# A small projection done in fp32 during the choice of experts, with another place for the seeds of the sums and another order of the weight ring

## The chip, the cores and the metric

The kernel runs on one core of a Trainium2 chip. The metric is the time of one execution on the device in microseconds (us); lower is better. The engines are TensorE (PE; its weight loads are PEld), VectorE (DVE), ScalarE (ACT), GpSimd (POOL) and SyncE (SP), which issues most of the weight transfers.

## What is computed

Two blocks act one after the other on 256 tokens of width 1024, all in fp32: a hybrid block (state-space mixer and block attention, then a mixture of experts, then a gate by a per-layer embedding), and a block of RWKV and convolution with a feed-forward layer. The part that the change touches:

```python
# x: after the mixer.  32 experts in 4 groups of 8, two chosen in a token's group
h = rms_norm(x, moe_norm_w)
x = x + hier_moe(h, w_router_group, b_router_group, w_router_expert,
                 b_router_expert, w_exp_gate, w_exp_up, w_exp_down)
gate = sigmoid(rms_norm(x, ple_norm_w) @ w_ple_gate)     # 1024 -> 1024
x = x + gate * (p @ w_ple)                               # p: 256 x 256, w_ple: 256 x 1024
return rms_norm(x, final_norm_w)
```

`p @ w_ple` depends on inputs alone.

## The kernel before

Most dense products are made in three passes. A weight piece of 512 KB (128 partitions x 1024 fp32) is loaded by `fetch` through SP's queue into a buffer `raw`; `split` makes a high half `whi` on ScalarE (L238) and the rest `wlo` on VectorE (L239); PE multiplies hi by hi, lo by hi and hi by lo in the faster fp32r form (L266, L284). Only products of plain fp32 tiles, such as transposes, gathers, the router and the experts, go to PE unsplit.

The program is written stage by stage, and a tile scheduler sets each engine's queue from that order, the buffers and the dependences. Each engine then runs its queue in order.

`mix1` is the first mixer. Its last product writes X1, the residual (256 tokens in two halves of 128); `hT_chunk` transposes it into two tiles `hT`. `route` multiplies hT by the router's weights `wr` (L794), chooses group and experts on VectorE (ending in `sel`, L819), and counts the tokens per expert with small matmuls on PE (the rank matmuls, L847). `moe` goes over 8 groups of 4 experts: `gather` makes a selection matrix `Pm` (L946) and collects 32 tokens for each expert with 32 matmuls (L955) into `xg`; 64 matmuls (L986) make gate and up; silu and product; 32 matmuls (L1007) make the down product; `slots` (L965) makes the weights `PT`, by which L1015 adds the results to four PSUM sums `acc`. These sums begin with X1 itself: four fp32 matmuls of X1 with the identity, the seeds (L938). After the gate and up products of the first group, all engines branch around `overflow` (L861), which is for an expert with more than 32 tokens; it isn't taken here.

The experts' weights are 192 pieces of 512 KB, 16 of gate and up and 8 of down for each group, taken from HBM in the order of use. `expert_fetch` (L911) puts piece n into buffer n modulo 40 of a ring, `self.ring`. The first 38 pieces (`NFIRST`) are issued ahead of the router, each when the buffer's earlier user is done: the `mw` buffers at P12 and P6 of the mixer's order `PROG1`, the rest of 38 at the start of `moe`. From piece 38 on a piece is issued where its user stands in the program, and waits for its buffer:

```python
n.ring = [(mw, "mw")] * NEARLY + [(None, "a8")] * 16 + [(raw, "raw")] * 4
n.ring += [(wsp, "whi"), (wsp, "wlo")] * 3 + [(mw, "mw")] * 2
```

After the experts, X1 is taken from the sums (L1023) and squared (L304). `ple` transposes it into `xh` and `xl` (L377, L378), calls `ple_proj`, which splits p and w_ple and makes U = p @ w_ple with 24 fp32r matmuls (L1045), and multiplies by `w_pg` (`toks`, 8 pieces of 12 matmuls, L284); sigmoid, product with U and sum follow (L1069 to L1071), then the norm into the second block.

Of the kernel before, what the change touches and what calls it, by code (L numbers as in the profile page):

```python
# [9 lines left out]
F32 = mybir.dt.float32  # L10
# [157 lines left out]
class Net:  # L168
# [524 lines left out]
    def mix1(self):  # L693
# [41 lines left out]
        for c in range(2):  # L735
# [9 lines left out]
            self.hT_chunk(X1, c)  # L745
        self.X1 = X1
# [40 lines left out]
    def route(self, hT, r):  # L787
# [4 lines left out]
        for tt in range(2):  # L792
            for kt in range(8):
                PE.matmul(ps[:, tt, :], hT[kt // 4][:, kt % 4, tt * 128:tt * 128 + 128], wr[:, kt, :], start=(kt == 0),  # L794
                          stop=(kt == 7))
        L = self.c1.tile([128, 2, 36], F32, name="L")
# [59 lines left out]
    def overflow(self, acc, comb, rank, cnti):  # L856
# [4 lines left out]
        with tc.If(cv > 32):  # L861
# [6 lines left out]
            hT = self.hT  # L868
            gu, pt = [self.bank(tag="B") for _ in range(2)], self.bank((128, 256), "B")
            with tc.For_i(0, 8) as q:  # L870
                for e in range(4):
                    for kt in range(8):
                        w = self.t2(s="wf")
                        nc.gpsimd.dma_start(w, a["w_gu"][bass.ds(q, 1), kt, e // 2, :, e % 2, :].rearrange("o p n -> (o p) n"))
                        for tt in range(2):
                            PE.matmul(gu[tt], hT[kt // 4][:, kt % 4, tt * 128:tt * 128 + 128], w, start=(kt == 0), stop=(kt == 7))
# [47 lines left out]
    def moe(self):  # L924
# [3 lines left out]
        self.expert_early(NFIRST - self.wi)  # L928
# [5 lines left out]

        acc = [[self.bank(tag="A", s="acc") for _ in range(2)] for _ in range(2)]
        for h in range(2):
            for tt in range(2):
                PE.matmul(acc[tt][h], self.ident, X1[:, tt, 512 * h:512 * h + 512], start=True, stop=False,  # L938
                          skip_group_check=True)
# [37 lines left out]
        nxt = gather(0)  # L977
        for q in range(8):
# [9 lines left out]
            if q == 0:  # L988
                self.overflow(acc, comb, rank, cnti)
                PT = slots(q, Pm)  # L990
# [27 lines left out]
        self.p = self.t2((128, 2, 256), s="p")  # L1018
        nc.sync.dma_start(self.p, a["pT"])
# [9 lines left out]
    def ple_proj(self):  # L1029
# [3 lines left out]
        self.U = U = self.a8(shape=(128, 2, 1024), s="U")  # L1033
        ph, pl = (self.t2((128, 2, 256), F32R, s="ps") for _ in range(2))
        S.activation(ph, self.p, AF.Copy)
        V.tensor_sub(pl, self.p, ph.bitcast(F32))
        for c in range(2):
            hi, lo = self.split(self.fetch(a["w_ple"][c]))
            for tt in range(2):
                ts = slice(128 * tt, 128 * tt + 128)  # L1040
                ps = self.bank(tag="B")
                n = 0
                for kt in range(2):
# [676 lines left out]
```

## Time and profile before

| | us |
|---|---|
| median of 3 runs | 1257.74 (1257.6 to 1259.7) |
| the profiled execution | 1260.09 |
| its span, first to last instruction | 1258.4 |
| PE busy | 1131.2 |
| VectorE busy | 745.1 |
| ScalarE busy | 511.5 |

The rows further down are from the profiled execution; its times count from the first instruction. Its mean granted TensorE clock is 0.955 of full speed. Matmuls overlap in PE, so a row's duration is longer than the distance to the next one, and an fp32 matmul can stand as two records.

### The profile page before, as it was taken

To read this page: it belongs to the slowest core of one execution; us is meant where nothing else is said; L and a number is where in the kernel's file an instruction comes from. 1 tells how busy PE (TensorE), PEld (TensorE's weight loads), DVE (VectorE), ACT (ScalarE), POOL (GpSimd) and SP (SyncE) were. 2 spreads that over 40 slices of the span, in tenths; PEclk is the share of its full clock that TensorE was granted. 3 is DMA by queue.
4 is the path that set the end of the run, shared out by engine and by line. 5 is a ranking of instruction groups with operands and counts; after the bars stand their busy time and mean duration, and the time that the engine had idled before them with its cause. 6 is when DMAs were issued, how large, how long until landed. Compare 5 with 4: busy or idle time off the path is not lost.

```text
span 1258.4 us, 20687 instructions
## 1 busy us (share of the span) xinstructions
PE 1131.2 (90%) x8211; PEld 887.1 (70%) x8211; DVE 745.1 (59%) x1513; ACT 511.5 (41%) x881; POOL 119.7 (10%) x126
## 2 busy tenths in 40 slices
PE   5999999999979988878789899998749999999996
PEld 5988976667754433216687798887736797999995
DVE  4777677656532111106846799889884366656555
ACT  4643644544411000006536535556215335545453
POOL 0002330001000000000200501014200000000000
PEclk9999999999979999998889899998857999999998
DMA  8743555327769999994353365122420136555552
GB/s 300 277 162 104 155 179 167 120 98 288 272 258 409 409 409 409 409 408 146 116 184 132 98 183 157 52 93 84 150 60 2 35 108 233 179 189 191 189 187 99
DMA packets 82981, 242.26 MB, mean 193 GB/s; under 512 B 24160, under 2 KB 24416, under 8 KB 82496
## 3 DMA queue, kind: packets, MB, share of 16 engines
q1 hardware_dynamic: 80224, 231.11, 51.3%
q0 software_dynamic: 2224, 8.90, 2.6%
q8 instruction: 66, 1.08, 0.4%
q10 hardware_dynamic: 432, 0.89, 0.2%
q14 instruction: 35, 0.29, 0.1%
HBM read 234.31 MB, written 4.46 MB: 190 GB/s over the span
## 4 chain that ended last, share of the span: by engine, by line
PE 47%; DVE 11%; DMA 5%; ACT 3%; issue 2%; POOL 1%; DVEq 0%; ACTq 0%; POOLq 0%; SPq 0%
PE ps L266 17%; PE acc L284 7%; DVE cv L1454 4%; PE ps L986 3%; PE ps L1007 3%; DMA we<-in_w_gu 3%; PE ps L284 2%; DVE wlo L239 2%; PE ps L1586 2%; PE ps L955 2%; DMA we<-in_w_dn 2%; PE acc L1015 2%; PE ps L1304 1%; ACT whi L238 1%; PE ps L1045 1%
## 5 line engine op out<-in xcount | busy, mean ns | idle before, releaser
L239 DVE TENSOR_TENSOR wlo<-raw,whi 128x1024 fp32r<-128x1024 f32 (+1 forms) x230 | 291.7, 1272 | 157.9 <-ACT whi L238 155.9
L238 ACT ACTIVATE whi<-raw 128x1024 fp32r<-128x1024 f32 (+1 forms) x230 | 242.2, 1055 | 289.7 <-PE ps L266 141.4
L266 PE MATMUL ps<-xh,whi 128*128 128x256 f32 x760 | 222.7, 293 | 9.1 <-DVE rkv L1135 4.2
L266 PE MATMUL ps<-xh,wlo 128*128 128x256 f32 x760 | 219.6, 291 | 1.6 <-DVE wlo L239 1.6
L266 PE MATMUL ps<-xl,whi 128*128 128x256 f32 x760 | 220.8, 291 | 0.0
L266 PEld LDWEIGHTS ps<-xh,whi 128*128 128x128 f32 x760 | 149.2, 196 | 14.7 <-DVE rkv L1135 4.7
L266 PEld LDWEIGHTS ps<-xh,wlo 128*128 128x128 f32 x760 | 148.4, 196 | 4.6 <-issue 1.8
L266 PEld LDWEIGHTS ps<-xl,whi 128*128 128x128 f32 x760 | 149.4, 197 | 3.1 <-issue 2.3
L1454 DVE SCALAR_TENSOR_TENSOR cv<-up,par,cv 128x256 f32<-128x256 f32 x232 | 106.3, 498 | 0.6
L986 PE MATMUL ps<-we,xg 128*32 128x512 f32 x512 | 75.9, 597 | 4.8 <-DMA we<-in_w_gu 4.8
L266 PE MATMUL ps<-h,whi 128*128 128x256 f32 x256 | 72.2, 282 | 0.0
L266 PE MATMUL ps<-l,whi 128*128 128x256 f32 x256 | 71.9, 281 | 0.0
L266 PE MATMUL ps<-h,wlo 128*128 128x256 f32 x256 | 71.9, 281 | 0.0
L284 PE MATMUL ps<-wlo,xh 128*128 128x512 f32 x128 | 50.7, 397 | 1.8 <-DVE wlo L239 1.8
L284 PE MATMUL ps<-whi,xh 128*128 128x512 f32 x128 | 50.9, 398 | 0.0
L284 PE MATMUL ps<-whi,xl 128*128 128x512 f32 x128 | 50.5, 394 | 0.0
L284 PE MATMUL acc<-wlo,fh 128*128 128x512 f32 x128 | 49.9, 390 | 0.0
L284 PE MATMUL acc<-whi,fl 128*128 128x512 f32 x128 | 49.9, 390 | 0.0
L284 PE MATMUL acc<-whi,fh 128*128 128x512 f32 x128 | 49.8, 389 | 0.0
L1007 PE MATMUL ps<-we,gT 128*32 128x512 f32 x256 | 44.1, 600 | 6.2 <-DVE gT L1001 3.5
L986 PEld LDWEIGHTS ps<-we,xg 128*32 128x32 f32 x512 | 16.4, 109 | 46.6 <-issue 24.8
L266 PEld LDWEIGHTS ps<-h,whi 128*128 128x128 f32 x256 | 48.2, 188 | 0.6 <-ACT re L1634 0.2
(477 smaller groups left out, 2025.2 us busy)
## 6 DMA issues: line engine op xcount, KB each, us to landing
we<-in_w_gu SPq DMA_DIRECT2D x128, 512.0 KB, 10.2
we<-in_w_dn SPq DMA_DIRECT2D x64, 512.0 KB, 10.2
raw<-in_w_ff SPq DMA_DIRECT2D x64, 512.0 KB, 4.2
raw<-in_w_g SPq DMA_DIRECT2D x32, 512.0 KB, 3.2
raw<-in_w_qkv SPq DMA_DIRECT2D x24, 512.0 KB, 3.2
raw<-in_w_rkv SPq DMA_DIRECT2D x24, 512.0 KB, 3.3
raw<-in_w_o SPq DMA_DIRECT2D x16, 512.0 KB, 5.8
raw<-in_w_glu SPq DMA_DIRECT2D x16, 512.0 KB, 3.2
```

The lines of the kernel that those rows point to most:

```text
L238: nc.scalar.activation(hi, r, AF.Copy)
L239: nc.vector.tensor_sub(lo, r, hi.bitcast(F32))
L266: pin(nc.tensor.matmul(out[f], w[:, k, c], x[:, kt, :], start=(kt == 0 and j == 0), stop=(kt == 7 and j == 2)))
L284: pin(nc.tensor.matmul(out[tt], x[:, x0 + k, s], w[:, k, :], start=(kt == 0 and j == 0), stop=(kt == last and j == 2)))
L955: PE.matmul(ps[:, f, :], X1[:, tt, ft * 128:ft * 128 + 128], Pm[:, tt, :], start=(tt == 0), stop=(tt == 1))
L986: PE.matmul(gu[32 * e:32 * e + 32, :], xg[:, kt, 32 * e:32 * e + 32], w[e // 2][:, e % 2, :], start=(kt == 0), stop=(kt == 7), skip_group_ ...
L1007: PE.matmul(py[h][32 * e:32 * e + 32, :], gT[:, kt * 128 + 32 * e:kt * 128 + 32 * e + 32], w[e // 2][:, e % 2, :], start=(kt == 0), stop=( ...
L1015: PE.matmul(acc[tt][h], PT[:, tt * 128:tt * 128 + 128], y, start=False, stop=(q == 7 and n == 1), skip_group_check=True)
L1045: PE.matmul(ps, x[:, kt, ts], ww[:, kt, :], start=(n == 0), stop=(n == 5))
L1304: PE.matmul(ps[H(h), q, :], lhs[H(h), q, :], r, start=True, stop=True)
L1454: pin(nc.vector.scalar_tensor_tensor(last, x[:, j:j + 256], self.P("cw", 8 * j + ft), o, op0=ALU.mult, op1=ALU.add))
L1586: pin(nc.tensor.matmul(out[f], r[:, k, 128 * f:128 * f + 128], z[:, kt, :], start=(kt == 0), stop=(kt == 7)))
```

## The change

- **Projection.** `ple_load` issues pT (256 KB) and w_ple (two pieces of 512 KB) at the end of `mix1`. `ple_proj` is called twice in `route`, right after the router's matmuls, and makes U with 8 plain fp32 matmuls from the raw tiles. U lies in a pool of its own until `ple` is done. The splits of p and w_ple and the 24 matmuls after the experts are gone.
- **Overflow.** The branch's body transposes X1 itself, so `hT` is free once the router's matmuls are done.
- **Seeds.** The four seeds are written behind the first group's gate and up matmuls, ahead of the branch.
- **Ring.** 38 buffers instead of 40 (`NEARLY` 10), in another order: the three pairs of split buffers come before `hT`'s two and the `raw` four. Of the first 38 pieces two are issued after the first gather.

```diff
@@ mix1
             self.hT_chunk(X1, c)
+        self.ple_load()
         self.X1 = X1
@@ route, behind the router's matmuls
+        self.ple_proj(0)
+        self.ple_proj(1)
         L = self.c1.tile([128, 2, 36], F32, name="L")
@@ overflow
-            hT = self.hT
...
+                        hk = self.t2((128, 256), s="hk")
                         for tt in range(2):
-                            PE.matmul(gu[tt], hT[kt // 4][:, kt % 4, tt * 128:tt * 128 + 128], w, start=(kt == 0), stop=(kt == 7))
+                            PE.transpose(ht[:, tt * 128:tt * 128 + 128], X1[:, tt, kt * 128:kt * 128 + 128], self.ident)
+                        V.tensor_scalar(hk, ht, self.P("mnw", kt), None, op0=ALU.mult)
+                        for tt in range(2):
+                            PE.matmul(gu[tt], hk[:, tt * 128:tt * 128 + 128], w, start=(kt == 0), stop=(kt == 7))
@@ moe
-        self.expert_early(NFIRST - self.wi)
+        self.expert_early(NFIRST - 2 - self.wi)
...
         acc = [[self.bank(tag="A", s="acc") for _ in range(2)] for _ in range(2)]
-        for h in range(2):
-            for tt in range(2):
-                PE.matmul(acc[tt][h], self.ident, X1[:, tt, 512 * h:512 * h + 512], start=True, stop=False,
-                          skip_group_check=True)
...
         nxt = gather(0)
+        self.expert_early(2)
...
             if q == 0:
+
+                for h in range(2):
+                    for tt in range(2):
+                        PE.matmul(acc[tt][h], self.ident, X1[:, tt, 512 * h:512 * h + 512], start=True, stop=False,
+                                  skip_group_check=True)
                 self.overflow(acc, comb, rank, cnti)
...
-        self.p = self.t2((128, 2, 256), s="p")
-        nc.sync.dma_start(self.p, a["pT"])
...
-    def ple_proj(self):
+    def ple_load(self):
+
+        nc, a = self.nc, self.a
+        self.pp = self.act.tile([128, 1024], F32, name="pp", tag="P", bufs=2)[:, 0:512].rearrange("p (k t) -> p k t", k=2)
+        nc.sync.dma_start(self.pp, a["pT"])
+        self.wp = [self.fetch(a["w_ple"][c]) for c in range(2)]
+
+    def ple_proj(self, c):
 
         nc, a = self.nc, self.a
         V, PE, S = nc.vector, nc.tensor, nc.scalar
-        self.U = U = self.a8(shape=(128, 2, 1024), s="U")
-        ph, pl = (self.t2((128, 2, 256), F32R, s="ps") for _ in range(2))
-        S.activation(ph, self.p, AF.Copy)
-        V.tensor_sub(pl, self.p, ph.bitcast(F32))
-        for c in range(2):
-            hi, lo = self.split(self.fetch(a["w_ple"][c]))
-            for tt in range(2):
-                ts = slice(128 * tt, 128 * tt + 128)
-                ps = self.bank(tag="B")
-                n = 0
-                for kt in range(2):
-                    for x, ww in ((ph, hi), (pl, hi), (ph, lo)):
-                        PE.matmul(ps, x[:, kt, ts], ww[:, kt, :], start=(n == 0), stop=(n == 5))
-                        n += 1
-                S.activation(U[:, tt, 512 * c:512 * c + 512], ps, AF.Copy)
+        U = self.U
+        for tt in range(2):
+            ts = slice(128 * tt, 128 * tt + 128)
+            ps = self.bank(tag="B")
+            for kt in range(2):
+                PE.matmul(ps, self.pp[:, kt, ts], self.wp[c][:, kt, :], start=(kt == 0), stop=(kt == 1))
+            S.activation(U[:, tt, 512 * c:512 * c + 512], ps, AF.Copy)
@@ ple
-        self.ple_proj()
@@ constants and net
-NEARLY = 12
+NEARLY = 10
...
-            n.ring = [(mw, "mw")] * NEARLY + [(None, "a8")] * 16 + [(raw, "raw")] * 4
-            n.ring += [(wsp, "whi"), (wsp, "wlo")] * 3 + [(mw, "mw")] * 2
+            n.ring = [(mw, "mw")] * NEARLY + [(None, "a8")] * 16 + [(wsp, "whi"), (wsp, "wlo")] * 3
+            n.ring += [(mw, "mw")] * 2 + [(raw, "raw")] * 4
```

What stands in the engines' queues shows how the scheduler placed it. First PE's queue in the router, before: L794 are the router's matmuls, L757 the last transposes into hT, L938 the seeds, L847 the rank matmuls (an x3 or x4 is a run of equal rows).

```order
L938 MATMUL acc_3317<-X_2984,const_82 128x512
L757 MATMUL ps_3172<-const_82,X_2984 128x128 x3
L757 MATMUL ps_3179<-const_82,X_2984 128x128 x3
L938 MATMUL acc_3319<-X_2984,const_82 128x512
L794 MATMUL ps_3227<-wr,hT_2987 128x36 x3
L938 MATMUL acc_3318<-X_2984,const_82 128x512
L794 MATMUL ps_3227<-wr,hT_2987 128x36
L794 MATMUL ps_3227<-wr,hT_2986 128x36 x4
L794 MATMUL ps_3227<-wr,hT_2987 128x36 x4
L938 MATMUL acc_3320<-X_2984,const_82 128x512
L847 LDWEIGHTS ltb
L847 MATMUL ps_3303<-sel,ltb 128x32
```

And of the changed kernel, where the router's matmuls are L795, the transposes L758, and L1052 is the projection (`pp` is p transposed, `raw` the weights w_ple):

```order
L1052 MATMUL ps_3250<-raw_3188,pp 128x512
L758 MATMUL ps_3172<-const_86,X_2984 128x128 x3
L758 MATMUL ps_3179<-const_86,X_2984 128x128 x3
L1052 MATMUL ps_3250<-raw_3188,pp 128x512
L795 MATMUL ps_3233<-wr,hT_2987 128x36 x3
L1052 MATMUL ps_3254<-raw_3188,pp 128x512
L795 MATMUL ps_3233<-wr,hT_2987 128x36
L795 MATMUL ps_3233<-wr,hT_2986 128x36 x4
L795 MATMUL ps_3233<-wr,hT_2987 128x36 x4
L1052 MATMUL ps_3254<-raw_3188,pp 128x512
L1052 MATMUL ps_3258<-raw_3190,pp 128x512 x2
L1052 MATMUL ps_3262<-raw_3190,pp 128x512 x2
```

Three projection matmuls stand where three seeds stood, and five more behind them; the rank matmuls (L850) come next. Behind these, and ahead of the first gather, stands one seed (L996); the other three stand behind the first group's gate and up products, ahead of the branch.

Next SP's queue at the end of the mixer, before (`raw` with in_w_o are the mixer's last weights, `we` the experts' pieces):

```order
L230 DMA raw_3130<-in_w_o 128x1024
L230 DMA raw_3148<-in_w_o 128x1024
L911 DMA we_3192<-in_w_gu 128x1024
L911 DMA we_3194<-in_w_gu 128x1024
L911 DMA we_3196<-in_w_gu 128x1024
L911 DMA we_3198<-in_w_gu 128x1024
L911 DMA we_3200<-in_w_gu 128x1024
L911 DMA we_3202<-in_w_gu 128x1024
L911 DMA we_3204<-in_w_gu 128x1024
L911 DMA we_3186<-in_w_gu 128x1024 x2
```

And of the changed kernel, where L919 is the issue of an expert's piece:

```order
L230 DMA raw_3148<-in_w_o 128x1024
L1040 DMA pp<-in_pT 128x512
L230 DMA raw_3188<-in_w_ple 128x1024
L230 DMA raw_3190<-in_w_ple 128x1024
L919 DMA we_3214<-in_w_gu 128x1024
L919 DMA we_3216<-in_w_gu 128x1024
L919 DMA we_3198<-in_w_gu 128x1024
L919 DMA we_3200<-in_w_gu 128x1024
L919 DMA we_3202<-in_w_gu 128x1024
L919 DMA we_3192<-in_w_dn 128x1024 x2
```

The three loads of the projection stand behind the mixer's last weights, in front of fourteen early pieces.

Last ScalarE's queue at the start of the embedding's stage, before (`junk` are the squares of X1, `xh` the high half of its transpose, `p_` and `raw_4868`, `raw_4890` belong to the projection, `raw_4918` is the first piece of w_pg):

```order
L304 ACTIVATE junk_4789,ss_4776<-X_2984 128x512
L377 ACTIVATE xh_4810<-ps_4812,par 128x256
L377 ACTIVATE xh_4810<-ps_4821,par 128x256
L377 ACTIVATE xh_4810<-ps_4830,par 128x256
L377 ACTIVATE xh_4810<-ps_4812,par 128x256
L377 ACTIVATE xh_4810<-ps_4839,par 128x256
L377 ACTIVATE xh_4810<-ps_4821,par 128x256
L377 ACTIVATE xh_4810<-ps_4830,par 128x256
L1035 ACTIVATE ps_4864<-p_4777 128x512
L238 ACTIVATE whi_4870<-raw_4868 128x1024
L377 ACTIVATE xh_4810<-ps_4839,par 128x256
L238 ACTIVATE whi_4892<-raw_4890 128x1024
```

And of the changed kernel, where `raw_5021` and `raw_5039` are the first two pieces of w_pg:

```order
L304 ACTIVATE junk_4935,ss_4930<-X_2984 128x512
L238 ACTIVATE whi_5023<-raw_5021 128x1024
L304 ACTIVATE junk_4938,ss_4930<-X_2984 128x512
L304 ACTIVATE junk_4941,ss_4930<-X_2984 128x512
L377 ACTIVATE xh_4962<-ps_4964,par 128x256
L377 ACTIVATE xh_4962<-ps_4973,par 128x256
L377 ACTIVATE xh_4962<-ps_4982,par 128x256
L377 ACTIVATE xh_4962<-ps_4964,par 128x256
L377 ACTIVATE xh_4962<-ps_4991,par 128x256
L377 ACTIVATE xh_4962<-ps_4973,par 128x256
L377 ACTIVATE xh_4962<-ps_4982,par 128x256
L238 ACTIVATE whi_5041<-raw_5039 128x1024
```

The projection's three splits are gone, and the first piece of w_pg is split between the squares, ahead of `xh`.

## Rows read from the trace of the kernel before

**Rows 1.** The page's busy times of the engines over the span.

```profile
PE 1131.2 (90%) x8211; PEld 887.1 (70%) x8211; DVE 745.1 (59%) x1513; ACT 511.5 (41%) x881; POOL 119.7 (10%) x126
```

**Rows 2.** Stretch 380 to 565: its length, each engine's busy us (count), PEclk, DMA share, GB/s.

```profile
380.00:565.00 185.00, 161.16 (x1002) 60.71 (x994) 29.89 (x79) 14.95 (x29) 0.84 (x2) 1.00 1.03 409
```

**Rows 3.** Chain that ended last, 540 to 640, in order of time: start, us, what.

```profile
552.49 10.16 DMA we<-in_w_dn
...
575.57 0.95 ACT whi L238
...
576.57 8.02 PE ps L1045 x24
```

**Rows 4.** Stretches around the router's choice, columns as in rows 2.

```profile
344.00:348.00 4.00, 4.00 (x29) 3.27 (x28) 2.04 (x10) 1.57 (x2) 0.00 (x0) 1.00 0.97 370
...
349.00:350.00 1.00, 0.00 (x0) 0.00 (x0) 0.86 (x5) 0.00 (x0) 0.00 (x0) 1.00 1.04 414
...
353.00:354.00 1.00, 0.38 (x2) 0.41 (x3) 0.96 (x5) 0.00 (x0) 0.00 (x0) 0.50 0.03 12
354.00:359.00 5.00, 5.00 (x25) 5.00 (x25) 2.42 (x15) 0.21 (x1) 0.00 (x0) 0.50 0.00 2
```

**Rows 5.** Timeline of SP, 360 to 385: start, us, engine, line, op, tiles, count.

```profile
361.24 0.81 SPq L911 DMA_DIRECT2D we<-in_w_gu  x2
```

**Rows 6.** Timeline of PE, 360 to 400, with idle time before and its releaser.

```profile
360.15 7.07 PE L986 MATMUL ps<-we,xg 128*32 128x512 f32 x64
372.26 1.03 PE L965 MATMUL ps<-comb,Pm 128*128 128x33 f32 x4 [5.04 <-PEq L861]
...
379.84 3.64 PE L1007 MATMUL ps<-we,gT 128*32 128x512 f32 x32 [0.90 <-DVE gT L1001]
...
393.14 3.84 PE L955 MATMUL ps<-Pm,X 128*128 128x128 f32 x32
```

**Rows 7.** Timeline of PE, 346 to 362.

```profile
347.89 1.10 PE L938 MATMUL acc<-X,const 128*128 128x512 f32 x2
352.58 0.19 PE L847 MATMUL ps<-sel,ltb 128*128 128x32 bf16 x1 [3.59 <-DVE sel L819]
...
353.62 6.60 PE L955 MATMUL ps<-Pm,X 128*128 128x128 f32 x32 [0.73 <-DVE Pm L946]
```

**Rows 8.** Timeline of PE, 574 to 609.

```profile
584.43 0.39 PE L284 MATMUL ps<-whi,xh 128*128 128x512 f32 x1
```

**Rows 9.** Line L284, 583 to 610: ns min/median/max, first and last start in us.

```profile
L284 PE MATMUL ps<-wlo,xh x32: 388/388/388, 584.9 to 606.2; 128*128 128x512 f32 x32
```

**Rows 10.** Tile acc, 340 to 352, columns as in rows 9.

```profile
L938 PE MATMUL acc<-X,const x8: 592/594/677, 342.0 to 348.4; 128*128 128x512 f32 x8
```

**Rows 11.** Tile we, 300 to 360: issues on SP, and us from issue to landing.

```profile
L911 SPq DMA_DIRECT2D we<-in_w_gu x14: 327/400/1178, 325.0 to 345.0; - x14
...
DMA to landing us min/median/max: 3.1/6.4/9.6
```

**Rows 12.** Waits of SP, 365 to 385: waiter, releaser, us in total, times, longest.

```profile
SPq L911 <- PE ps L1007: 1.3, 1, 1.3
```

**Rows 13.** Groups by line, 568 to 612: busy us, mean ns, idle before and releasers.

```profile
L239 DVE TENSOR_TENSOR wlo<-raw,whi 128x1024 fp32r<-128x1024 f32 x13 | 15.9, 1224 | 8.7 <-ACT whi L238 8.5
L238 ACT ACTIVATE whi<-raw 128x1024 fp32r<-128x1024 f32 x13 | 13.7, 1062 | 7.3 <-PE ps L284 4.6 <-issue 1.0 <-ACT g L1069 1.0
```

**Rows 14.** Timeline of ACT, 568 to 580.

```profile
571.09 0.63 ACT L304 ACTIVATE junk<-X 128x512 bf16<-128x512 f32 x1 [0.89 <-DVE X L1023]
...
572.38 2.68 ACT L377 ACTIVATE xh<-ps,par 128x256 fp32r<-128x256 f32 x7
```

**Rows 15.** Timeline of DVE, 568 to 580.

```profile
572.98 3.02 DVE L378 SCALAR_TENSOR_TENSOR xl<-ps,par,xh 128x256 fp32r<-128x256 f32 x7
```

**Rows 16.** Stretches of 1 us in the embedding's stage, columns as in rows 2.

```profile
575.00:576.00 1.00, 0.00 (x0) 0.00 (x0) 1.00 (x5) 1.00 (x3) 0.00 (x0) 0.50 0.00 0
...
581.00:582.00 1.00, 1.00 (x5) 0.79 (x4) 0.46 (x3) 0.13 (x1) 0.00 (x0) 0.83 0.81 225
```

More of the change, by code (lines that the diff above doesn't have):

```diff
@@ L867, in overflow @@
             V.memset(wo[1], 0.0)
-            hT = self.hT
-            gu, pt = [self.bank(tag="B") for _ in range(2)], self.bank((128, 256), "B")
+            X1 = self.X1
+            gu, pt = [self.bank(tag="B") for _ in range(2)], self.bank(tag="B")
+            pt, ht = pt[:, 0:256], pt[:, 256:512]
             with tc.For_i(0, 8) as q:
@@ L1671, in ffn @@
                 nc.sync.dma_start(a["out"][128 * tt:128 * tt + 128, s], XC[:, tt, s])
-PROG1 = "X0 X1 T Z0 Z1 W D0 D1 Y5 Y6 Y0 Y1 Y2 v1 r Y3 Y4 Y7 N q0 q1 R0 k0 S k1 R1 v0 B1 A0 P12 A1 A2 B0 A3 A4 A5 A6 A7 P6 C0 C1"
+PROG1 = "X0 X1 T Z0 Z1 W D0 D1 Y5 Y6 Y0 Y1 Y2 v1 r Y3 Y4 Y7 N q0 q1 R0 k0 S k1 R1 v0 B1 A0 P10 A1 A2 B0 A3 A4 A5 A6 A7 P6 C0 C1"
 PROG = "K0 L K2 K1 A0 U0 B0 U1 M0 M0 M0 M0 M0 O0 R0 R1 R2 A1 G0 B1 G2 M1 M1 M1 M1 G1 G3 M1 C0 C1 C2 C3 C4 C5 C6 C7 O1 S D1 D0"
 STEPS = "m0 p0,m1 p1 s0,m2 p2 s1,m3 p3 s2,s3"
-NEARLY = 12
+NEARLY = 10
 NFIRST = 38
@@ L1683, in net @@
     n = Net(ctx, tc, a, off, tap)
+    pu = ExitStack()
+    n.U = pu.enter_context(n.pool("pu", 1, side="right")).tile([128, 2, 1024], F32, name="U")
     with n.pool("mw", NEARLY + 2, side="right") as n.mw, n.pool("c1") as n.c1:
@@ L1699, in net @@
                 n.ple()
+                pu.close()
             n.mix2(late)
```

## Prediction, made before the changed kernel ran

> **What bounds the kernel now.** I looked first at which engine fills the span: TensorE (PE) is busy for 1131.2 of 1258.4 us [rows 1]. Such an average hides stages with other limits, so I then read tables by stretch and the chain of work that ended last, at the two places that the change touches.
>
> Between 380 and 565 us the experts' weights bound the time: the DMA share is 1.03 at 409 GB/s, while PE is busy for 161 of 185 us [rows 2]. A piece of 512 KB takes 524,288 B / 409 GB/s = 1.28 us there. It needs 10.2 us from issue to landing [rows 3], so 10.2 / 1.28 = 8 are under way at once. The chain goes through these landings, not through PE. So in this stage only one thing counts: when the stream starts, and whether it runs without a hole.
>
> It starts late. The 38 pieces that fit before the choice of experts have landed by 354, and from 354 to 359 the DMA share is 0.00 [rows 4]. Refilling begins at 361.24 [rows 5], after the first group's matmuls, which start at 360.15, give their buffers back [rows 6]. What decides that start is the router: from 348.99 (347.89 + 1.10) PE waits 3.59 us for the choice `sel`, runs the rank matmuls, and then gathers tokens for 6.60 us [rows 7]. The gather is slow because the granted clock is 0.50 from 353 to 359, right after the idle stretch [rows 4]. The same 32 matmuls for the third group, at 393.14, take 3.84 us [rows 6].
>
> After the last expert the embedding's stage hangs on PE and on what feeds it. ScalarE's first seven `xh` are done at 575.06 (572.38 + 2.68 [rows 14]); then the chain goes through the splits of `p` and `w_ple` and through 8.02 us of the 24 projection matmuls L1045 [rows 3]. Only then come the 96 matmuls of `w_pg`, from 584.43 [rows 8]. One in three of them (32) starts between 584.9 and 606.2 [rows 9], so one matmul takes (606.2 - 584.9) / 31 / 3 = 0.229 us.
>
> **The change, part by part.** I keep the clock times of the kernel before, and say how far each event moves.
>
> (1) *Eight fp32 matmuls for the projection in the router.* They have the form of the four seeds (128x512, two records each). The last seed takes 1.10 us [rows 7]; the starts of its two records are 0.51 apart (347.89 and 348.4 [rows 7, 10]), which makes 1.02 for each in a row of them. Three projection matmuls stand exactly where three seeds stood and cost nothing new. The fourth takes the last seed's place at 347.89, and four more follow it. At 1.02 the five last until 353.0, against 352.58 for the first rank matmul: 0.4 us late. The bounds: they end in time if one takes 0.94 or less, and at 1.10 they are 0.8 late. I take 0.3.
>
> Their inputs, 1.31 MB, go through SP's queue ahead of the last early pieces. Loads of that stretch took at most 9.6 us to land [rows 11]. They use the buffers into which the first two `we` of the stretch went, the first of them at 325.0; with 4 us for the second they land at 325 + 4 + 9.6 = 338.6 at the worst, ahead of the first use at 342.0 [rows 10]. Their transfer (3.2 us at 409 GB/s) pushes the last early pieces back, into the stretch in which DMA stands idle [rows 4]. Those pieces belong to the second group, which comes after the down products at 379.84. Without the idle stretch this part would cost 3.2 us.
>
> (2) *The gather.* PE no longer stands idle for 3.59 us ahead of it. I expect the clock to stay at the full level, 2.4 GHz, and the gather to take 3.84 instead of 6.60 us: 2.8 us. The one seed between the rank matmuls and the gather (1 us) lies beside VectorE's work on Pm, for which PE waited 0.73 us [rows 7]; it may cost 0.3. Parts (1) and (2) together bring the first group's start forward by 2.8 - 0.3 - 0.3 = 2.2 us; 1.4 to 2.8 by the bounds, 0 or a loss of 0.6 if the clock falls all the same.
>
> (3) *Three seeds ahead of the overflow branch, and a ring of 38 instead of 40.* PE reaches the branch at 367.2 (360.15 + 7.07), stands there for 5.04 us, and the down products start at 379.84, behind slots, gather and silu [rows 6]. Three seeds of about 1 us put PE at the branch at 367.2 - 2.2 + 3.0 = 368.0, so the down products start at 380 or a little later, no earlier.
>
> The Trainium skill ("Runtime: NRT & Kernel Launch", Instruction fetch mechanics) says that a taken branch to instructions that are not already at hand stops the engine until they are fetched; by that rule the seeds cannot hide in the 5.04 us, as the sum has it. The trace names PE's own sequencer for the wait, and no other engine, which agrees. Were it a wait for another engine, the seeds would fit into it, and the down products would start up to 2.2 us sooner.
>
> The stream now runs 2.2 us earlier and needs the first down buffer two pieces (2.6 us) earlier. SP waited 1.3 us for it before [rows 12]; now it waits for about 1.3 + 2.2 + 2.6 + 0.2 = 6.3 us. The pieces under way cover 10.2 - 6.3 = 3.9 us, and one piece into an idle queue takes 3.1 [rows 11]. No hole, by 0.8 us. I book 0.2, with bounds 0 and 2. So the stream, and all behind it, moves by 2.2 - 0.2 = 2.0 us.
>
> (4) *The embedding's stage.* Gone are the splits of `p` and `w_ple` and the 8.02 us of matmuls. The first `w_pg` piece takes the buffer in which the first `w_ple` came, which was loaded beside the last experts, and is split by ScalarE while that waits for X (0.89 us idle [rows 14]). So its first matmul can start with the first `xh`, at about 573.0 instead of 584.43. Then the feed sets the pace for two pieces. `xl` starts at 572.98 and comes every 0.43 us (3.02 for seven [rows 15]), eight by 576.4, so piece 0 ends at about 576.5. ScalarE splits piece 1 after the seven `xh` (575.06 + 1.06 = 576.1), VectorE adds 1.22 [rows 13]: 577.4, and piece 1 ends at about 579.5. From there each of six pieces takes 12 x 0.229 = 2.74 us: 579.5 + 16.5 = 596.0 instead of 606.2, a gain of 10.2 us. Bounds: with no waits at all 573.0 + 21.9 = 594.9, 11.3 us; half clock (the first rival) 6.8.
>
> What follows, and every later stage, keeps its order on all engines, and the loads of the next stage wait for the splits of `w_pg`, so they move with it. The four copies to `U` (0.6 us each, by the 128x512 form on ScalarE [rows 14]) lie in the router, where ScalarE idles, as at 349 [rows 4]; without that cover 2.5 us.
>
> Two edits come at nothing: the two `we` loads fewer in the early part, whose buffers no PE wait of that part rests on, and the longer body of the branch, which is not taken.
>
> **Sum.** -2.0 - 10.2 = -12.2 us. The profiled execution took 1260.09 us (span 1258.4, 1.7 around it), so a profile of after should show about 1247.9. The median of the runs of before is 2.35 below the profiled one: 1257.74 - 12.2 = 1245.5 us.
>
> **Rivals.**
>
> *The clock falls in the first `w_pg` pieces.* Before, PE was idle from the transposes' end until 576.57, and the clock stood at 0.50 at 575 and came back at 581 [rows 16]. Now PE works in that stretch, but in bits, paced by `xl` and `wlo`. If that is too little, pieces 1 and 2 run at 1.2 GHz, at twice 0.229 for each: over 6.8 us of half clock 3.4 us are lost. Gain 6.8 there, 8.8 in all: 1249 us. If the router's clock falls as well, 1251. The Trainium skill ("TensorE: Matmul & The Clock Gate", HAM oscillation) describes how short bursts of matmuls between waits leave the engine at half rate; this trace shows that only after whole idle stretches. Against it: 24 matmuls, 5.5 us of work, fall into the 6.5 us from 573. Chance 0.19.
>
> *The hole in the ring.* If the down products of the first group come one or two us later than I think, the stream halts for that long: the router's gain is eaten, only the 10.2 stays, 1247.5. Chance 0.10; it lies inside the range.
>
> *The earlier start brings no earlier end.* If the splits bound the 96 matmuls, the removed projection gains little: 1256 to 1260 with -2 to +2 us. VectorE, the fuller of the two, needs 8 x 1.22 + 3.4 + about 5 for gates and sums = 18 us [rows 13, 15], against 22 of PE. Chance 0.05.
>
> *Slower.* The projection matmuls stand in PE's queue ahead of the router's second half. If `w_ple` landed late, the router, and with it the stream, would wait one for one. This turns the sign when the landing comes 12 us after 342, at 354; at 358 it would give about 1261. By the slowest load of that stretch it comes by 338.6, so 0.03.
>
> **Chances.** The forecast, with a range of its own of 1243 to 1248: 0.61; the clock 0.19; the hole 0.10; no earlier end 0.05; slower 0.03; more than 15 us gained 0.02. About 0.2%, 2.5 us, is what can be told from no change. Faster: 0.61 + 0.19 + 0.10 + 0.02 = 0.92; the case of no earlier end is mostly same, so same 0.04, slower 0.04. The range reaches over the clock's case and leaves out what is beyond: 1242 to 1251.
>
> **What would show it.** In a profile of after: the projection matmuls without a gap up to about 353; clock 1.00 from 344 to 367; gather near 3.9 us; refilling from about 359; the down products of the first group still near 380, and a DMA share of 1.03 with no dent near 383; no projection after the experts; the first `w_pg` matmul within 1 us of the first `xh`, and the 96 done in 23 us. I am wrong if the clock shows 0.50 in either place, if the stream has a hole near 383, or if the router waits for `w_ple`.

## The result, and the profile after

| | before | after |
|---|---|---|
| median, us | 1257.93 (4 runs, 1257.6 to 1259.7) | 1245.64 (4 runs, 1243.36 to 1248.44) |
| ratio, 95% interval | | 0.990 (0.9876 to 0.9925) |
| profiled execution, us | 1260.09 | 1243.36 |
| its span, us | 1258.4 | 1241.7 |

The changed kernel is 12.3 us faster. The two profiled executions lie further apart, 16.7 us (1260.09 is above the median of before, 1243.36 the lowest of after). So I cut both into five stretches at four events of PE (times from its timelines, in us):

| stretch | before | after | difference |
|---|---|---|---|
| start of the span to the first rank matmul | 352.58 | 351.36 | -1.22 |
| to the first group's first matmul | 7.57 | 4.75 | -2.82 |
| to the end of the last down product | 208.18 | 208.62 | +0.44 |
| to the end of the last `w_pg` matmul | 38.23 | 27.57 | -10.66 |
| to the end of the span | 651.85 | 649.38 | -2.47 |

The three in the middle hold the change: -13.0 us. The first and the last row differ as much between kernels that do the same work there. Over all the profiles of this study the last stretch takes 644.9 to 651.9 us in the four without the change (mean 648.7), and 646.2 to 650.8 in the eight with it (mean 649.2); the first takes 350.9 to 352.7 and 350.4 to 354.2. The second and the third row spread as well, as the experiments show; the fourth repeats to a few hundredths in the kernels with the change that leave it alone.

Now the rows. Of PE's whole busy time the page of after shows the same as before [rows 1]; the gain isn't in the amount of work:

```profile
PE 1131.5 (91%) x8203; PEld 881.1 (71%) x8203; DVE 742.3 (60%) x1510; ACT 508.8 (41%) x878; POOL 121.1 (10%) x126
```

The stretches of after that answer to rows 2, 4 and 16 (columns as there):

```profile
344.00:348.00 4.00, 4.00 (x23) 2.85 (x23) 1.90 (x11) 0.20 (x2) 0.00 (x0) 1.00 1.02 407
...
349.00:350.00 1.00, 1.00 (x4) 0.48 (x3) 0.86 (x5) 0.46 (x1) 0.00 (x0) 1.00 1.01 414
...
353.00:354.00 1.00, 1.00 (x11) 1.00 (x10) 0.72 (x7) 0.21 (x1) 0.00 (x0) 1.00 1.02 410
354.00:359.00 5.00, 5.00 (x48) 2.92 (x50) 2.17 (x8) 0.00 (x0) 0.00 (x0) 1.00 0.47 158
380.00:385.00 5.00, 5.00 (x42) 2.69 (x44) 1.70 (x8) 0.71 (x2) 0.00 (x0) 1.00 1.03 410
380.00:565.00 185.00, 162.97 (x984) 61.15 (x982) 30.95 (x81) 14.30 (x29) 0.85 (x2) 0.98 1.01 404
...
575.00:576.00 1.00, 1.00 (x6) 0.84 (x5) 1.00 (x3) 0.00 (x0) 0.00 (x0) 1.00 0.84 319
```

PE works through 349:350, where it stood before, and the clock column reads 1.00 where it read 0.50, in the gather (353 to 359) and at 575. From 354 to 359 the DMA share is 0.47 where it was 0.00: the early pieces that the projection's loads pushed back run there, and the refill begins at 357.2 instead of 361.24 [rows 5]. The stream of the weights keeps its rate (404 against 409 GB/s) and has no dent at 380:385, where the first down products give back their buffers.

PE's timeline of after, in the router, at the branch and at the embedding (answers to rows 6, 7 and 8):

```profile
346.68 4.54 PE L1052 MATMUL ps<-raw,pp 128*128 128x512 f32 x10
351.36 0.18 PE L850 MATMUL ps<-sel,ltb 128*128 128x32 bf16 x1
...
352.43 3.75 PE L958 MATMUL ps<-Pm,X 128*128 128x128 f32 x32
356.11 7.07 PE L990 MATMUL ps<-we,xg 128*32 128x512 f32 x64
363.12 2.84 PE L996 MATMUL acc<-X,const 128*128 128x512 f32 x6
368.38 0.60 PE L968 MATMUL ps<-comb,Pm 128*128 128x33 f32 x4 [2.43 <-PEq L864]
...
375.97 3.64 PE L1016 MATMUL ps<-we,gT 128*32 128x512 f32 x32 [0.90 <-DVE gT L1010]
...
563.68 1.05 PE L1016 MATMUL ps<-we,gT 128*32 128x512 f32 x4
...
569.30 0.73 PE L284 MATMUL ps<-whi,xh 128*128 128x512 f32 x2 [0.32 <-ACT xh L377]
```

No row of the router waits any more; the wait at the branch has shrunk from 5.04 to 2.43 us; and `w_pg` starts 4.57 us after the last down product's end (563.68 + 1.05), without a projection between. Not everything behind the branch is at full clock: the column reads 0.50 or near it from 369 to 372.

ScalarE's timeline of after at the embedding shows the first `whi` between the squares, ahead of all `xh` (rows 14 before):

```profile
566.50 1.05 ACT L238 ACTIVATE whi<-raw 128x1024 fp32r<-128x1024 f32 x1
...
568.79 2.65 ACT L377 ACTIVATE xh<-ps,par 128x256 fp32r<-128x256 f32 x7
571.32 2.02 ACT L238 ACTIVATE whi<-raw 128x1024 fp32r<-128x1024 f32 x2
```

And the waits of SP at the refill, where before 1.3 us stood [rows 12]:

```profile
SPq L919 <- PE ps L1016: 3.6, 1, 3.6
```

### The profile page after: what moved, and what is told of

Same layout as the page of the kernel before. It is cut to its first block, busy times and chain, and to the rows that moved or that the text cites. A ratio compares the mean times of both kernels' runs of the same rounds, so it can differ in the third digit from the quotient of the medians.

```text
span 1241.7 us, 20668 instructions
## 1 busy us (share of the span) xinstructions
PE 1131.5 (91%) x8203; PEld 881.1 (71%) x8203; DVE 742.3 (60%) x1510; ACT 508.8 (41%) x878; POOL 121.1 (10%) x126
## 4 chain that ended last, share of the span: by engine, by line
PE 35%; DMA 16%; DVE 13%; ACT 2%; issue 2%; POOL 1%; DVEq 0%; SPq 0%; ACTq 0%; POOLq 0%
PE ps L266 14%; DMA we<-in_w_gu 8%; PE acc L284 7%; DMA we<-in_w_dn 4%; DVE cv L1459 4%; DVE wlo L239 3%; PE ps L1591 2%; PE ps L1309 1%; DMA raw<-in_w_o 1%; PE ps L284 1%; DMA raw<-in_w_pg 1%; PE ps L1016 1%; ACT whi L238 1%; PE ps L958 1%; PE ps L990 1%
## 5 line engine op out<-in xcount | busy, mean ns | idle before, releaser
L266 PEld LDWEIGHTS ps<-xh,whi 128*128 128x128 f32 x760 | 147.9, 195 | 10.7 <-issue 2.5
L284 PE MATMUL ps<-wlo,xh 128*128 128x512 f32 x128 | 50.8, 400 | 1.8 <-DVE wlo L239 1.8
L284 PE MATMUL ps<-whi,xh 128*128 128x512 f32 x128 | 50.9, 399 | 0.3 <-ACT xh L377 0.3
L284 PE MATMUL ps<-whi,xl 128*128 128x512 f32 x128 | 50.5, 395 | 0.0
L284 PE MATMUL acc<-wlo,fh 128*128 128x512 f32 x128 | 49.9, 390 | 0.0
L284 PE MATMUL acc<-whi,fl 128*128 128x512 f32 x128 | 49.9, 390 | 0.0
L284 PE MATMUL acc<-whi,fh 128*128 128x512 f32 x128 | 49.8, 389 | 0.0
L266 PEld LDWEIGHTS ps<-l,whi 128*128 128x128 f32 x256 | 48.2, 188 | 0.2
## 6 DMA issues: line engine op xcount, KB each, us to landing
we<-in_w_gu SPq DMA_DIRECT2D x128, 512.0 KB, 10.2
we<-in_w_dn SPq DMA_DIRECT2D x64, 512.0 KB, 10.2
```

What stands on the lines that cost most here:

```text
L266: pin(nc.tensor.matmul(out[f], w[:, k, c], x[:, kt, :], start=(kt == 0 and j == 0), stop=(kt == 7 and j == 2)))
L284: pin(nc.tensor.matmul(out[tt], x[:, x0 + k, s], w[:, k, :], start=(kt == 0 and j == 0), stop=(kt == last and j == 2)))
```

## Experiments

The theory that I tested: the time falls for two reasons that don't depend on each other. PE is kept busy ahead of the gather, so the gather runs at 2.4 GHz; and the projection is off the path behind the experts. The rivals: the number form (fp32 for three passes) is what saves time; the clock isn't bound to the idle stretch; seeds ahead of the branch, and a shorter ring, cost what the router gains.

### after_again: the changed kernel once more

> The changed kernel itself once more, for a narrower interval and a second profile. Theory (10.2 us from the embedding's stage, 2 from the router): 1245.6, 12 us below before, and in the profile a gather of 3.8 us and the first w_pg matmul within 1 us of the first xh. Rival (the two profiled executions differ by 16.7 us, so more than these two stages gained): about 1241.5. In the profile the early load stage and the loads of w_l in the second block show whether their 4 us come again or were chance.

Measured: 1243.81 us (ratio 0.9882, 0.9853 to 0.9911). Gather 3.75 us, rank matmul to first group 4.75 us, last down product to last `w_pg` matmul 27.57 us: these stretches repeat to the hundredth, while the total varies by 8 us over six runs. From the first group to the last down product it is 210.00 us here, 1.4 more than in after: that stretch doesn't repeat so well, and a difference of one or two us in it shows nothing.

### before_fill: only the idle stretch filled

```diff
+        for i in range(4):
+            fl = self.bank(tag="B", s="fill")
+            PE.matmul(fl, self.ident, self.X1[:, i % 2, 0:512], start=True, stop=True)
         L = self.c1.tile([128, 2, 36], F32, name="L")
```

> The kernel before with four more fp32 matmuls in the router whose result nobody reads; they fill PE's idle 3.6 us ahead of the choice. Theory (the clock falls because PE idles, and the first group's start sets the stream of weights): clock 1.00 through the gather, gather 3.8 us, first group 2.4 us earlier, total -2.4, about 1255.5. Rival A (the stream of weights is not moved by it, or loses it in a hole): 1257.9 with a fast gather. Rival B (the clock falls all the same): gather 6.6 us and +0.5.

Measured: 1255.37 us (0.9986, 0.9970 to 1.0002). PE's timeline of this kernel:

```profile
348.93 3.60 PE L941 MATMUL acc<-X,const 128*128 128x512 f32 x8
352.67 0.18 PE L850 MATMUL ps<-sel,ltb 128*128 128x32 bf16 x1
...
353.68 3.81 PE L958 MATMUL ps<-Pm,X 128*128 128x128 f32 x32 [0.73 <-DVE Pm L949]
```

```profile
350.00:356.00 6.00, 5.12 (x32) 3.38 (x31) 4.83 (x30) 0.42 (x2) 0.00 (x0) 1.00 0.28 115
```

The rank matmuls start where they did before [rows 7], but PE does not stand idle ahead of them, the clock reads 1.00, and the gather takes 3.81 instead of 6.60 us. From the rank matmuls to the first group it is 4.75 us, as in after: work that nobody reads gives the router's whole gain. The medians differ by about 2 us, but the interval reaches over 1, so the total alone doesn't show it.

### after_gap: the change with the idle stretch put back

```diff
         self.ple_proj(0)
-        self.ple_proj(1)
+        nc.gpsimd.memset(self.U[:, :, 512:1024], 0.0)
...
+                keep = self.pin()
                 for h in range(2):
                     for tt in range(2):
-                        PE.matmul(acc[tt][h], self.ident, X1[:, tt, 512 * h:512 * h + 512], start=True, stop=False,
...
+                        keep(PE.matmul(acc[tt][h], self.ident, X1[:, tt, 512 * h:512 * h + 512], start=True, stop=False,
...
```

> The changed kernel with the second half of the projection left out (that half of U is zero) and all four seeds held behind the first group's matmuls, so that PE idles ahead of the choice again; the embedding's stage is as in the changed kernel. Theory: idle 3.6 us, clock 0.50, gather 6.6 us, first group 2.4 later than in the changed kernel, total +2.4, about 1248. Rival (the gain of the router's stage is not the clock's): 1245.6.

Measured: 1246.53 us (0.9909, 0.9885 to 0.9933), 2.7 above after_again beside it, with intervals that overlap; the stretch is what tells. PE's timeline and one stretch of this kernel:

```profile
352.71 0.21 PE L850 MATMUL ps<-sel,ltb 128*128 128x32 bf16 x1 [3.58 <-DVE sel L822]
...
353.75 5.27 PE L958 MATMUL ps<-Pm,X 128*128 128x128 f32 x32 [0.73 <-DVE Pm L949]
```

```profile
351.00:352.00 1.00, 0.00 (x0) 0.00 (x0) 0.92 (x6) 0.06 (x1) 0.00 (x0) 0.50 1.06 430
```

The wait of 3.58 us is that of before, and the clock falls within it. The gather takes 5.27, not 6.60: the clock fell and came back sooner in this execution (1.00 from 357 on; before, from 360). From the rank matmuls to the first group it is 6.25 us, 1.5 more than in after. So the filling and the clock are tied from both sides. How much the half clock costs depends on when it is given back: the gather took 6.60 in before, 6.30 in before_fp32 and 5.21 in before_no_proj, whose routers are the same, so 1.4 to 2.8 us more than at full clock (3.81 in before_fill).

### before_no_proj: only the late projection gone

```diff
-        self.p = self.t2((128, 2, 256), s="p")
-        nc.sync.dma_start(self.p, a["pT"])
...
-        self.ple_proj()
+        self.U = self.a8(shape=(128, 2, 1024), s="U")
+        nc.gpsimd.memset(self.U, 0.0)
```

> The kernel before, with the product of p and w_ple left out (U is filled with zeros by GpSimd), nothing else changed. Theory: the embedding's stage alone gives 10.2 us (bounds 9 to 11.3), so about 1247.7, and the router's stage stays as before: gather 6.6 us. Rival (the splits of w_pg bound its 96 matmuls, so the earlier start brings little): -2, 1256.

Measured: 1251.12 us (0.9953, 0.9935 to 0.9972), 3.4 above the theory. The embedding's stage takes 30.43 us: 7.8 less than before, not 10.7. PE's and ScalarE's timelines show where the rest is:

```profile
572.92 0.50 PE L284 MATMUL ps<-whi,xh 128*128 128x512 f32 x1 [2.35 <-ACT whi L238]
```

```profile
570.38 1.55 ACT L377 ACTIVATE xh<-ps,par 128x256 fp32r<-128x256 f32 x4
571.80 1.07 ACT L238 ACTIVATE whi<-raw 128x1024 fp32r<-128x1024 f32 x1
```

Here the scheduler put the first split of `w_pg` behind six `xh`, so PE waits 2.35 us for it, and the next matmuls take 0.63 us each instead of 0.39. Leaving the projection out isn't enough: the split must also stand ahead of the `xh`, as it does in after. The gather took 5.21 us here and not the 6.6 of the theory, with the same 3.58 us of idle time ahead of it.

### before_fp32: the fp32 form at the old place

```diff
-        ph, pl = (self.t2((128, 2, 256), F32R, s="ps") for _ in range(2))
-        S.activation(ph, self.p, AF.Copy)
-        V.tensor_sub(pl, self.p, ph.bitcast(F32))
...
-            hi, lo = self.split(self.fetch(a["w_ple"][c]))
+            w = self.fetch(a["w_ple"][c])
...
-                    for x, ww in ((ph, hi), (pl, hi), (ph, lo)):
-                        PE.matmul(ps, x[:, kt, ts], ww[:, kt, :], start=(n == 0), stop=(n == 5))
-                        n += 1
+                    PE.matmul(ps, self.p[:, kt, ts], w[:, kt, :], start=(kt == 0), stop=(kt == 1))
```

> The kernel before with the projection left in its place after the experts, but as 8 plain fp32 matmuls on unsplit p and w_ple. It tells the form of the product from its place. Theory: PE needs 8 x 1.02 = 8.2 us instead of 8.0, but waits for no split and can begin at the end of the last group, in the 4 us in which PE idled; the 96 w_pg matmuls then start about 4 us earlier and the clock does not fall: -4, about 1253.5. Rival A (the place is all, the form nothing): 0. Rival B (the form is all): -10.

Measured: 1257.78 us (1.0011, 0.9990 to 1.0032). PE's timeline and a stretch of this kernel:

```profile
574.19 10.07 PE L1040 MATMUL ps<-raw,p 128*128 128x512 f32 x16 [2.15 <-issue]
```

```profile
576.00:580.00 4.00, 4.00 (x6) 1.69 (x5) 2.43 (x8) 0.60 (x1) 0.00 (x0) 0.50 0.37 125
```

The projection starts 6.4 us after the last down product's end, 1.8 sooner than before (8.2, its start in [rows 3]), since nothing is split for it. PE still stands idle for 2.15 us ahead of it; for what, the profile doesn't show. And it takes 10.07 us, 2.05 more, much of it at half clock; the stage takes 38.45 us against 38.23. At this place the form alone gives nothing, where I expected 4 us. The place is what counts.

### after_no_branch and after_seeds_first: the branch and the seeds

after_no_branch leaves out the overflow branch; after_seeds_first writes the four seeds ahead of the first gather.

```diff
-                self.overflow(acc, comb, rank, cnti)
```

```diff
+        for h in range(2):
+            for tt in range(2):
+                PE.matmul(acc[tt][h], self.ident, X1[:, tt, 512 * h:512 * h + 512], start=True, stop=False,
+                          skip_group_check=True)
         nxt = gather(0)
...
-                for h in range(2):
-                    for tt in range(2):
-                        PE.matmul(acc[tt][h], self.ident, X1[:, tt, 512 * h:512 * h + 512], start=True, stop=False,
-                                  skip_group_check=True)
                 self.overflow(acc, comb, rank, cnti)
```

> The changed kernel with the overflow branch left out (no token overflows here). Theory (the stream of weights sets the end, and the branch's 6.8 us in PE's sequencer lie beside it): the down products of group 0 start 3 us earlier, the total stays within 1 us of the changed kernel. Rival (fetching instructions for the branch makes the 1.5 us hole that the stream has 3 to 10 us after the refill): the hole is gone and the total falls by 1.5.

> The changed kernel with all four seeds between the rank matmuls and the first gather, none ahead of the branch. Theory (PE's sequencer runs ahead of the array and fetches behind the branch while the array still works on the seeds, so the three seeds cost nothing there): first group's start 2.9 us later, time from there to the first down products unchanged at 19.8 us with PE's idle time at the branch back at 5 us, total +2.9 against the changed kernel. Rival (as the prediction had it, seeds ahead of the branch are paid in full): from the first group's start to the down products 17 us instead of 19.8, and the total by the stream's start, +2.9 as well or less.

Measured: 1244.02 (0.9885, 0.9857 to 0.9912) and 1246.34 us (0.9898, 0.9877 to 0.9919). First the rows of the branch on the sequencers of PE and VectorE, in after (duration in ns, then the start), and that of PE in before:

```profile
L864 DVEq COMPARE_BRANCH  x1: 72/72/72, 356.8 to 356.8; - x1
...
L864 PEldq COMPARE_BRANCH  x1: 6752/6752/6752, 361.2 to 361.2; - x1
```

```profile
L861 PEldq COMPARE_BRANCH  x1: 6863/6863/6863, 365.1 to 365.1; - x1
```

PE's timelines of after_no_branch and of after_seeds_first:

```profile
363.20 2.84 PE L996 MATMUL acc<-X,const 128*128 128x512 f32 x6
365.88 0.53 PE L968 MATMUL ps<-comb,Pm 128*128 128x33 f32 x4
```

```profile
359.15 7.07 PE L994 MATMUL ps<-we,xg 128*32 128x512 f32 x64
370.67 1.03 PE L968 MATMUL ps<-comb,Pm 128*128 128x33 f32 x4 [4.44 <-PEq L864]
```

On PE the branch lasts 6.8 us, on VectorE 0.07. In after it begins at 361.2, while the array has work until 365.96 (363.12 + 2.84). So the sequencer is some 4.8 us ahead of the array, and matmuls that are queued already run beside the branch. In before it is 2.1 us ahead (367.22 - 365.1). Counted from the first group's start it reaches the branch after 5.1 us in after and after 4.95 in before: the three seeds hardly hold it up. With three seeds there PE stands idle for 2.43 us, with none for 4.44 (after_seeds_first) or 5.04 [rows 6]. From the first group's start to its down products it is 19.86 us in after, 19.48 in after_seeds_first, 19.69 before, and 15.14 without the branch. Over all profiles it is 19.25 to 20.32 with three seeds there (five, mean 19.75) and 18.89 to 20.76 with none (five, mean 19.68): the three seeds cost nothing that can be told, not 3 us. Ahead of the gather they are paid for in full, 2.55 us: the first group starts at 359.15, 7.30 after its rank matmuls instead of 4.75. The totals of after and after_seeds_first aren't told apart.

Without the branch the down products come 4.7 us sooner after the first group's start; part of that is the second gather, which runs at full clock there. The last down product ends 206.97 us after the first group's start; in the five profiles with the branch, the change and 38 buffers it is 208.0 to 210.0. So 1 to 3 us of the 4.7 arrive there, and the total isn't told apart from that of after: the weights' stream, more than PE, sets the time here. The rival, a hole in the stream made by the branch, is small at most. After's stream and that of after_no_branch, in the ten us behind the refill:

```profile
358.00:368.00 10.00, 7.96 (x58) 2.36 (x46) 0.00 (x0) 0.00 (x0) 0.00 (x0) 1.00 0.96 347
```

```profile
358.00:368.00 10.00, 10.00 (x78) 4.74 (x71) 0.82 (x6) 0.95 (x2) 0.00 (x0) 1.00 0.95 363
```

The 16 GB/s between them are 160 KB in ten us, 0.4 us of the stream, not 1.5.

### after_ring39 and after_ring36: the length of the ring

```diff
-        cb = self.act.tile([128, 2, 384], F32, name="cb", tag="cb")
+        cb = self.act.tile([128, 1024], F32, name="cb", tag="cb")[:, 0:768].rearrange("p (k t) -> p k t", k=2)
...
-NFIRST = 38
+NFIRST = 39
...
-            n.ring = [(mw, "mw")] * NEARLY + [(None, "a8")] * 16 + [(wsp, "whi"), (wsp, "wlo")] * 3
+            n.ring = [(mw, "mw")] * NEARLY + [(None, "a8")] * 16 + [(lambda: n.act, "cb")] + [(wsp, "whi"), (wsp, "wlo")] * 3
```

```diff
-NEARLY = 10
-NFIRST = 38
+NEARLY = 8
+NFIRST = 36
```

Not shown: with 39 the pool of small tiles `sm` has 13 buffers instead of 14; with 36, `P10` in `PROG1` is `P8`.

> The changed kernel with one weight buffer more: a tile of the first mixer (cb) that is idle during the experts is enlarged by 1 KB to hold a piece, the ring has 39 buffers, and 39 pieces are issued ahead of the refill. Theory (DMA idles between the last early piece and the refill, 357.7 to 360.9 in the profile of after, so every further buffer ahead of the refill takes 1.28 us off the stream): -1.3 against the changed kernel, and in the profile the stream's end 1.3 us earlier relative to the first group's start. Rival (a hole at the first down products, which the ring now reaches 1.28 us later, or DMA bandwidth shared with the router's loads): 0.

> The changed kernel with two weight buffers fewer (NEARLY 8, 36 pieces ahead of the refill). Theory: two pieces more to fetch after the refill, +2.6; and the first down buffer is needed 2.6 us earlier, for which SP would wait 3.7 + 2.6 = 6.3 us against 10.2 us of pieces under way less 3.1 for a single one, so still no hole. Rival 1 (a hole as well): +4 or more. Rival 2 (the ring's size doesn't matter, as PE bounds the groups): 0.

Measured: 1247.66 (0.9914, 0.9887 to 0.9942) and 1248.58 us (0.9924, 0.9896 to 0.9952), beside 1244.02 for after_no_branch on the same chip. The three intervals overlap, so the stretch must tell. From the first group's start to the last down product's end it is 207.92 us with 39 buffers, 208.03 to 210.00 in the five profiles with 38 and the branch, 212.11 with 36. So the two pieces fewer cost 2.1 to 4.1 us, 1.1 to 2.0 each, beside the 1.28 that a piece takes in the stream; what the piece more gains isn't told from nothing. SP's wait for a down buffer hardly moves with 36 (3.6 in after), where 6.3 was expected:

```profile
SPq L919 <- PE ps L1016: 3.8, 1, 3.8
```

Whatever the 39th buffer gains is lost again behind the experts, where the stage takes 30.21 us instead of 27.57. ScalarE's timeline:

```profile
567.70 1.54 ACT L377 ACTIVATE xh<-ps,par 128x256 fp32r<-128x256 f32 x4
569.12 1.07 ACT L238 ACTIVATE whi<-raw 128x1024 fp32r<-128x1024 f32 x1
```

It is the picture of before_no_proj: the first split stands behind six `xh`. With 36 and 38 buffers it stands ahead of them. What makes the scheduler choose, the ring or the small buffer fewer, I have not settled.

### after_split2: two splits written ahead of the transposes

```diff
+        pre = [(2 * p, 2) + self.split(self.fetch(a["w_pg"][0][p], (128, 2, 512))) for p in range(2)]
...
-            for tt, ps in enumerate(self.toks(xh, xl, a["w_pg"][c])):
+            for tt, ps in enumerate(self.toks(xh, xl, a["w_pg"][c], pre=() if c else pre)):
```

Not shown: `toks` takes the pieces in `pre` first and splits the others as before.

> The changed kernel with the splits of the first two w_pg pieces written ahead of the transposes, so that ScalarE makes both before xh. It tests whether the feed paces the start of the 96 w_pg matmuls, as the prediction had it. Theory: the second piece no longer waits for seven xh and its own split; the stage from the last down product to the last w_pg matmul takes 26.5 instead of 27.6 us, total -1. Rival (the xh come later by the time of the second split, 1.06 us): the stage is as long as before or longer by up to 1, total 0 to +1.

Measured: 1247.54 us (0.9916, 0.9896 to 0.9935), not told apart from after. The stage takes 31.55 us, 4.0 longer than in after, against all that I expected. PE's timeline and a stretch of this kernel:

```profile
572.44 0.91 PE L289 MATMUL ps<-whi,xh 128*128 128x512 f32 x2 [1.26 <-ACT xh L382]
574.13 0.80 PE L289 MATMUL ps<-whi,xl 128*128 128x512 f32 x1 [0.79 <-DVE xl L383]
```

```profile
572.00:573.00 1.00, 0.56 (x2) 0.30 (x2) 0.92 (x4) 1.00 (x4) 0.00 (x0) 0.92 0.52 147
...
573.00:579.00 6.00, 5.21 (x13) 3.81 (x13) 5.10 (x12) 3.46 (x8) 0.00 (x0) 0.50 0.43 150
```

The second split pushes `xh` and `xl` back, and the scheduler put a third one between the first four `xh` and the last four. PE waits 1.26 us for `xh`. Over 572 to 573 the clock reads 0.92, and 0.50 from 573 to 579: so it fell behind that wait, ahead of the second one of 0.79 us (573.34 to 574.13). That is the prediction's first rival, at the place that it named, brought about by a small edit; in after PE waits at most 0.45 us at a time there, and the clock stays at 1.00.

## Why the prediction was right, step by step

The forecast was 1245.5 us; 1245.64 was measured. That the two agree to 0.1 us is luck: by its interval the gain lies between 9.4 and 15.6 us. By the prediction's own steps:

**(1) The projection in the router: right.** Eight matmuls fit: ten records took 4.54 us, 0.91 for each matmul, inside the bound of 0.94. The last ended at 351.22, `sel` at 351.30, so they were not late at all (0.3 booked). Nothing waited for `w_ple`, and the early pieces that its load pushed back ran in the stretch in which DMA stood idle before.

**(2) The gather: right.** 3.75 us at full clock (3.84 forecast), and the seed between cost nothing. The first group starts 2.82 us sooner after the rank matmuls; 2.2 was booked, with 2.8 as the bound. But 2.82 is one pair of executions. From the rank matmuls to the first group it is 4.75 us in all seven profiles with the stretch filled and at most one seed ahead of the gather, and 6.17 to 7.57 in the four with the stretch idle: 1.4 to 2.8 gained. before_fill and after_gap show the cause from both sides.

**(3) The seeds ahead of the branch: wrong, without weight in the sum.** The step took the seeds as paid in full, with down products "at 380 or a little later". They came at 375.97, that is 377.2 on the clock of before (this execution ran 1.22 us ahead by then). Right was that PE's own sequencer makes the wait. Wrong was to take the array's end of work (367.2) for the time at which PE reaches the branch, and so to conclude that nothing fits beside it: in before the sequencer was there at 365.1, and what stands in PE's queue ahead of the branch runs while its sequencer is in the branch. So the down products came 2.8 us sooner, near the 2.2 that the working gave for a wait on another engine, though it is none. The Trainium skill ("Runtime: NRT & Kernel Launch", Instruction fetch mechanics) says that behind a taken branch to instructions that are not at hand the engine cannot go on until they are fetched; the rows agree with that, and they show that it stops what comes after, not what is queued already. The wait of SP was therefore 3.6 and not 6.3 us, 2.7 less, about as much as the down products came sooner (380 - 377.2). No hole appeared near the first down products, with more room than the 0.8 us forecast; but the stream gained nothing from the earlier down products, as its own start and rate set the end. The +0.44 us of the pair can't be held against the 0.2 booked: this stretch takes 208.2 to 209.2 us in the kernels without the change, and 208.0 to 210.0 in those with it that keep its ring and its branch.

**(4) The embedding's stage: right, 10.7 instead of 10.2 us.** First `w_pg` matmul 0.5 us after the first `xh` starts; 96 matmuls in 23.0 us (569.30 to 592.30), as forecast; the waits in the first two pieces came to 0.9 us, where the working had 1.0. Part of the 0.5 us more is a slip: the working set the end of the new matmuls, 596.0, against the start of the last old one, 606.2, and so left out one of 0.23 us. The step passed over a condition: the first split has to stand ahead of `xh`. I read it off the order of the changed kernel, but did not say what it was worth. before_no_proj and after_ring39 show 2.6 to 2.9 us, so a quarter of the stage's gain comes with that order and not with the projection itself.

**The rivals.** The clock's fall didn't happen, but was near: after_split2 has it, and its stage is 4.0 us longer with the waits. The hole in the ring did not happen (DMA share 1.03 at 380:385). No earlier end and a late `w_ple` are excluded by the rows above.

**The sum.** -2.82 + 0.44 - 10.66 = -13.0 us in the profiles, -12.2 forecast, -12.3 by the medians. One thing was not foreseen. At the start of the second block PE waited 3.9 to 4.2 us in the four kernels without the change, behind a VectorE that waited for a load (`raw` from `in_w_l`, 6.5 us to landing in before); in after PE waits 0.63 us there, and some 80 us behind the last `w_pg` matmul PE is 2.7 us ahead (82.89 us before and 80.18 after to the same matmul, the first one of `iv`). By the end of the span the means of the two kinds no longer differ (648.7 and 649.2). Why, and what gives it back, I did not try.

## What to carry to other kernels

Before hiding work in an idle stretch of PE, look at what comes behind it: a good part of such a stretch's price can lie in the clock after it (1.4 to 2.8 us here, behind 3.6 us of idle time), so that even unread work in the gap can pay (before_fill: 2.8 us at the place). A product of inputs alone belongs where PE waits for another engine, and here its number form mattered less than its place (before_fp32: nothing). Removing work from a path pays in full only if the next operand is ready by then: check in the engine's order where its preparation stands (2.6 to 2.9 us here).

## What the runs showed of the hardware

- A branch that all engines take around a block of skipped code held PE's sequencer for 6.2 to 7.2 us in eleven profiles, and VectorE's for 0.07 us. PE's sequencer reached it 2.1 us ahead of the array in before and 4.8 in after, so 2.84 us of matmuls ran beside it at no cost that the runs can tell.
- A wait of 1.26 us, behind shorter ones of 0.33, 0.45 and 0.16 us, was followed by 1.2 GHz for more than 6 us (after_split2); in after the same shorter ones and one of 0.32 us were not. The Trainium skill ("TensorE: Matmul & The Clock Gate", HAM oscillation) describes such a loss where bursts of matmuls wait for whole loads; here a shorter wait, for a tile that ScalarE makes, came ahead of it.
- Executions of one kernel range over up to 13 us (before: 1253.08 to 1263.79 in 23 runs, 1251.21 to 1264.34 in 17 others), while the embedding's stage repeats to 0.02 us in the five kernels with the change that leave it alone (27.55 to 27.57). A change of 2 us is read from its stage, not from the total.
